# A two-layer FFN block kernel: token blocks of the FFN's up-projection formed between its products, four tile pairs begun at its start, pools that wait tile by tile, and the first value product in a score bank

## The chip, the cores and the metric

The kernel runs on one core of a Trainium2 chip, as one program. The metric is the device time of one execution in microseconds; less is better. The names are those of the profile: PE is TensorE (PEld its weight loads), DVE is VectorE, ACT is ScalarE, POOL is GpSimd, SP is SyncE, which issues nearly all DMAs here.

## The reference

Two layers over 1024 tokens of width 1024, all in float32. Layer 0 mixes with a gated MLP and a multi-scale pool (the even mixer), layer 1 with two kinds of attention (the odd mixer). After each mixer stands the same feed-forward network, of width 2816, which this change is mostly about:

```
def conv_ffn(h, w_up, conv_w, conv_b, w_down):
    a, g = jnp.split(h @ w_up, 2, axis=-1)
    a = lax.conv_general_dilated(a, conv_w, window_strides=(1,), padding=((CONV_WIDTH - 1, 0),),
                                 dimension_numbers=('NWC', 'WIO', 'NWC'), feature_group_count=D_FF) + conv_b
    return (jax.nn.gelu(a) * g) @ w_down
...
        h = h + mix
        h = h + conv_ffn(rms_norm(h, norm_ffn[layer]), ffn_w_up[layer], ffn_conv_w[layer],
                         ffn_conv_b[layer], ffn_w_down[layer])
```

## The kernel before, in words

Activations lie transposed: features on the 128 partitions, tokens along the row. A half is 512 tokens. Every product of float32 operands is made of three matmuls on a high and a low part (`mm3`, L163 to L165): high times high, high times low, low times high. `split` (L174 a cast on ACT for the high part, L175 a subtraction on DVE for the low part) makes the two parts of an activation; weights get theirs from L348 and L352 in the FFN and L133 and L134 elsewhere.

The order on each engine is fixed when the program is built: a scheduler takes the order in which the code is written and places each engine's instructions from it. On the chip an engine works through its own list in order, and semaphores hold it where data or a buffer are not ready.

**The up-projection of the FFN** takes one pair of 128-column tiles (a tile of `a`, a tile of `g`) at a time, 22 pairs, numbered j, in each layer. The four products of a 2x2 block scheme are replaced by seven (a Strassen-like scheme): the tokens are the columns, the model width is cut in two, and the two token halves give blocks. Products 1 to 7 (`PRODUCTS`, each four steps of `mm3`, so 12 matmuls of 512 columns) multiply sums of weight tiles ("forms" 0 to 3 of a pair, made on DVE and split) by sums of token blocks:

- b11 and b21: the first half's tokens, scaled by the norm, in two halves of the width. They depend on the first half of the tokens alone.
- d, e, b22, t3, t4: sums and differences that need the second half's tokens too.

Product 1 uses b11, product 2 b21, product 3 d, product 4 e, product 5 b22, product 6 t3, product 7 t4. `read` takes the results out of PSUM: product 1 is copied by ACT (L412, f_x), 2 is added to it on DVE (L419, into the `a` row f_a), 3 copied (f_z), 4 copied (f_u) from the bank that product 1 opened, 5 added (L425), 6 added (L428). After product 7 come the convolution (L434 to L437) and the gate (L442, L443), which sends the pair's result to HBM.

The blocks are formed by `apply`, called twice. The call for half 0 makes b11 and b21; the call for half 1 makes d, e, b22, t3 and t4, all of them, before `up` begins. Each starts with `Norm.stats`: eight small matmuls that sum the squares over the partitions (ps_n, L209), a square root worked out on DVE in a chain of small steps (L212, L180 to L185), a copy (n_rb, L215) and matmuls that spread the result to all partitions (ps_b, L218). Then each 128-row tile is scaled (L309) in place, and blocks of 128x1024 are added (L322 for d, L326 for e, L331 for t3, L335 for t4) and split.

In `up`, the first two pairs run together, product by product (1 of both, 2 of both, 3, 4, 5, 6, 7); from pair 2 on each pair runs alone in the order 1, 2, 4, 3, 6, 5, 7, with the next pair's forms made in between. The seven products of a pair use three PSUM banks: x is taken from the pool ps_mm (2 buffers), y and z from ps_mx (4 buffers).

**Before the first FFN** stands the even mixer's output projection (`out_proj`, ps_o); it calls `apply(0)`, then the second half's projection with `ahead` (the forms 0 and 1 of the pairs 0 and 1), then `apply(1)`. **Before the second FFN** stands the odd mixer's output projection, in the loop at the end of the program: for each half, eight accumulations (ps_o), then `ahead`, then `apply`.

**At the start of the odd mixer** (`odd_mixer`) the query and key projection (`Proj.half`, ps_qk) and the value projection (`Values.half`, ps_vv) both take their PSUM banks from ps_mm, of two buffers. ps_qk of the first half takes both; ACT copies them out (L660); then ps_vv comes. Ahead of those copies in ACT's list stand the casts (L174, `hph<-n_t`) of the second half's norm. The score banks (`ps_sc`) are of a pool of the odd mixer, and lie where the pools ps_mx0 and ps_sm0 of the stage before lay.

**Pools**: a pool that is opened where another was closed must wait until the old contents are out of use. In the kernel before, the pools of the FFN have `reuse_waits="tile"` (a tile waits for those old tiles alone that lay in its place); the others don't.

Of the kernel before, what the change touches and what calls it, by code (L numbers as in the profile page):

```python
# [18 lines left out]
P = 128  # L19
# [41 lines left out]
def tile_block(  # L61
# [22 lines left out]
    const = ctx.enter_context(tc.tile_pool(name="const", bufs=1))  # L84
    dram = ctx.enter_context(tc.tile_pool(name="dram", bufs=1, space=DRAM))
    wraw_p = ctx.enter_context(tc.tile_pool(name="wraw", bufs=2))
    wsp_p = ctx.enter_context(tc.tile_pool(name="wsp", bufs=4))
    hn_p = ctx.enter_context(tc.tile_pool(name="hn", bufs=1))
    ps_mm = ctx.enter_context(tc.tile_pool(name="ps_mm", bufs=2, space=PSUM))
# [174 lines left out]
    class FFN:  # L264
        def __init__(self, layer, stack):
            self.layer = layer
            hp = stack.enter_context(tc.tile_pool(name=f"ffh{layer}", bufs=1, reuse_waits="tile"))
            self.raw_p = stack.enter_context(tc.tile_pool(name=f"ffr{layer}", bufs=4, reuse_waits="tile"))
            self.np = tc.tile_pool(name=f"ffn{layer}", bufs=1, reuse_waits="tile")
# [21 lines left out]
        def apply(self, half):  # L291
            pb, _ = self.norm.stats(half * HF)
            H = self.H
            if half == 0:
                self.X = self.blocks("x", F32R)
            X = self.X
            self.B = {
                "b11": ([hph[m][0] for m in range(2)], [hpl[m][0] for m in range(2)]),
                "b21": ([hph[m + 2][0] for m in range(2)], [hpl[m + 2][0] for m in range(2)]),
                "b22": ([hph[m + 2][1] for m in range(2)], [hpl[m + 2][1] for m in range(2)]),  # L300
                "d": ([hph[m][1] for m in range(2)], [hpl[m][1] for m in range(2)]),
                "e": (X[0], X[1]),
                "t3": (X[2], X[3]),
            }

            def scaled(m):
                for kt in (2 * m, 2 * m + 1):
                    t = self.hT[kt][half]
                    V.scalar_tensor_tensor(t, t, pcol(PC_FFN[self.layer] + kt), pb, op0=ALU.mult, op1=ALU.mult)  # L309

            def put(name, m, src):
                hi, lo = self.B[name]
                split(hi[m], lo[m], src)

            if half == 0:
                for m in range(4):
                    scaled(m)
                    put("b11" if m < 2 else "b21", m % 2, H[m][0])
                return
# [908 lines left out]
```

## Time and profile before

| what | value |
|---|---|
| median of 3 runs | 2398.79 us |
| lowest, highest | 2397.45, 2400.97 us |
| the profiled execution's own time | 2396.34 us |
| its span, from the first to the last instruction | 2394.6 us |
| PE busy | 2307.8 us, 96% of the span |
| DVE busy | 1552.0 us, 65% |
| ACT busy | 954.8 us, 40% |
| mean granted PE clock | 0.988 |

PE is busy nearly always; the windows view tells where it is not, and where its clock was granted at less than 1.00. The first FFN's up-projection begins at about 260 us of the span, the odd mixer at about 938 us, the second FFN's at about 1685 us.

A row of the windows view gives a stretch of the span, its length, then busy time and number of instructions of PE, PEld, DVE, ACT and POOL, then the granted PE clock, the share of busy DMA engines and GB/s. A row of the timeline gives the start, the length (of a group of xN instructions, all together), the engine, the line, the operation with output and inputs and, in brackets, how long the engine sat idle before it and who released it. Matmul rows overlap, since the pipeline takes in the next while the last drains: what counts is the distance from start to start.

### The profile page before, as it was taken

What the parts mean: (1) busy time and instruction counts of PE and PEld (TensorE: products, weight loads), DVE (VectorE), ACT (ScalarE), POOL (GpSimd) and SP (SyncE); (2) the same over time, 40 slices, a digit from 0 to 9 for tenths busy, and PEclk for the clock granted to TensorE, in tenths of its full rate; (3) what the DMA queues carried; (4) which work ended last, traced back from release to release, by engine and by line L of the source; (5) the groups of instructions that cost most, each with busy time, mean ns of one, the idle gap of its engine ahead of it and who ended that gap; (6) DMA issues with size and microseconds to landing.
All of it is one profiled execution on the core that took longest, in us unless ns stands there. A gap on an engine that the chain in (4) does not pass through costs nothing.

```text
span 2394.6 us, 30695 instructions
## 1 busy us (share of the span) xinstructions
PE 2307.8 (96%) x11652; PEld 1948.4 (81%) x11652; DVE 1552.0 (65%) x2957; ACT 954.8 (40%) x1549; POOL 9.2 (0%) x67
## 2 busy tenths in 40 slices
PE   7999899999999998999999999999699999999997
PEld 7888688888888887898888888878578888888887
DVE  6663976666674447355544788896986666675446
ACT  6231433343441113445544555663444333341111
POOL 0000000000000000000000000000000000000000
PEclk9999999999999999999999999999899999999998
DMA  4114132222273213122122131233322222263211
GB/s 139 62 55 165 36 97 88 79 80 80 88 244 107 89 50 108 55 76 79 60 69 73 37 103 54 75 124 135 134 89 88 88 80 80 86 235 119 88 36 71
DMA packets 174067, 221.60 MB, mean 93 GB/s; under 512 B 11104, under 2 KB 121952, under 8 KB 173920
## 3 DMA queue, kind: packets, MB, share of 16 engines
q1 hardware_dynamic: 173056, 218.61, 28.0%
q8 instruction: 91, 1.49, 0.3%
q10 hardware_dynamic: 864, 1.04, 0.2%
q14 instruction: 56, 0.46, 0.1%
HBM read 160.79 MB, written 52.53 MB: 89 GB/s over the span
## 4 chain that ended last, share of the span: by engine, by line
PE 82%; DVE 9%; ACT 4%; DMA 3%; issue 2%; SPq 0%; DVEq 0%; ACTq 0%
PE ps_d L163 7%; PE ps_d L164 7%; PE ps_d L165 7%; PE ps_x L163 6%; PE ps_x L165 6%; PE ps_x L164 6%; PE ps_z L165 3%; PE ps_z L164 3%; PE ps_z L163 3%; PE ps_qk L163 3%; PE ps_qk L165 3%; PE ps_qk L164 3%; PE ps_o L165 2%; PE ps_o L163 2%; PE ps_o L164 2%
## 5 line engine op out<-in xcount | busy, mean ns | idle before, releaser
L163 PE MATMUL ps_d<-hph,wh 128*128 128x512 f32 (+1 forms) x736 | 279.8, 380 | 0.0
L164 PE MATMUL ps_d<-hpl,wh 128*128 128x512 f32 (+1 forms) x736 | 279.7, 380 | 0.0
L165 PE MATMUL ps_d<-hph,wl 128*128 128x512 f32 (+1 forms) x736 | 279.6, 380 | 0.0
L544 DVE TENSOR_TENSOR x<-ps_d,x 128x512 f32<-128x512 f32 (+1 forms) x200 | 131.9, 666 | 184.9 <-PE ps_d L165 184.7
L134 DVE TENSOR_TENSOR wl<-raw,wh 128x1024 fp32r<-128x1024 f32 (+1 forms) x110 | 131.9, 1200 | 172.7 <-ACT wh L133 172.5
L133 ACT CAST wh<-raw 128x1024 fp32r<-128x1024 f32 (+1 forms) x110 | 113.3, 1036 | 261.8 <-PE ps_d L164 177.3
L348 ACT CAST wh<-q 128x1024 fp32r<-128x1024 f32 x88 | 92.4, 1050 | 247.9 <-PE ps_z L164 218.9
L352 DVE TENSOR_TENSOR wl<-q,wh 128x1024 fp32r<-128x1024 f32 x88 | 107.6, 1224 | 126.7 <-ACT wh L348 126.7
L165 PEld LDWEIGHTS ps_d<-hph,wl 128*128 128x128 f32 x736 | 138.4, 188 | 26.4
L163 PEld LDWEIGHTS ps_d<-hph,wh 128*128 128x128 f32 x736 | 138.4, 188 | 26.3
L164 PEld LDWEIGHTS ps_d<-hpl,wh 128*128 128x128 f32 x736 | 138.4, 188 | 25.9
L163 PE MATMUL ps_qk<-hph,wh 128*128 128x512 f32 x384 | 151.9, 396 | 0.0
L165 PE MATMUL ps_qk<-hph,wl 128*128 128x512 f32 x384 | 151.6, 395 | 0.0
L164 PE MATMUL ps_qk<-hpl,wh 128*128 128x512 f32 x384 | 151.5, 394 | 0.0
L163 PE MATMUL ps_z<-hph,wh 128*128 128x512 f32 x352 | 139.0, 397 | 7.1 <-ACT hph L174 6.6
L163 PE MATMUL ps_x<-x,wh 128*128 128x512 f32 x352 | 137.3, 391 | 4.8 <-ACT f_u L412 4.8
L165 PE MATMUL ps_z<-hph,wl 128*128 128x512 f32 x352 | 139.3, 396 | 1.0 <-DVE wl L352 1.0
L164 PE MATMUL ps_z<-hpl,wh 128*128 128x512 f32 x352 | 139.5, 396 | 0.7 <-DVE hpl L175 0.7
L164 PE MATMUL ps_x<-x,wh 128*128 128x512 f32 x352 | 137.3, 390 | 1.0 <-DVE x L175 1.0
L165 PE MATMUL ps_x<-x,wl 128*128 128x512 f32 x352 | 136.8, 389 | 0.0
L163 PE MATMUL ps_vv<-wh,hph 128*128 128x256 f32 x384 | 110.2, 287 | 10.2 <-ACT qk L660 10.2
L164 PE MATMUL ps_vv<-wl,hph 128*128 128x256 f32 x384 | 110.7, 288 | 0.0
(268 smaller groups left out, 5511.4 us busy)
## 6 DMA issues: line engine op xcount, KB each, us to landing
wr<-in_w_up SPq DMA_DIRECT2D x88, 512.0 KB, 4.1
a_dram<-h SPq DMA_DIRECT2D x44, 512.0 KB, 2.6
ar<-a_dram SPq DMA_DIRECT2D x44, 512.0 KB, 4.6
raw<-in_w_dn SPq DMA_DIRECT2D x44, 512.0 KB, 4.5
raw<-in_w_oin SPq DMA_DIRECT2D x36, 512.0 KB, 3.7
h_dram<-h SPq DMA_DIRECT2D x32, 256.0 KB, 4.8
x<-h_dram SPq DMA_DIRECT2D x32, 256.0 KB, 5.2
raw<-in_w_ein SPq DMA_DIRECT2D x12, 512.0 KB, 4.4
```

The source lines that it names most:

```text
L133: A.copy(wh, raw)
L134: V.tensor_sub(wl, raw, wh.bitcast(F32))
L163: T.matmul(ps, lh, rh, start=first, stop=False, skip_group_check=more)
L164: T.matmul(ps, lh, rl, start=False, stop=False, skip_group_check=more)
L165: T.matmul(ps, ll, rh, start=False, stop=last, skip_group_check=more)
L348: A.copy(t[0], src)
L352: V.tensor_sub(l, src, h.bitcast(F32))
L544: V.tensor_tensor(h, ps, h, op=ALU.add)
```

## The change

1. `FFN.apply(1)` no longer forms blocks; it only gets the norm's scale. A new method `block` forms one block of one index, and `up` calls it between the products, each block just ahead of the product that uses it.
2. Pairs 2 and 3 (`early`) run their products 1 and 2, which need b11 and b21 alone, in the first group too, before product 3 of any pair; their sum is kept in a small tile and copied to the `a` row when the pair's turn comes (`open_a`). Their raw `a` tiles are loaded and split by `ahead` in place of form 1 of the pairs 0 and 1, which moves into `up`; the whole of their raw tiles is loaded again later.
3. The up-projection takes its six banks once and hands them on in a list (`self.banks`): a product that opens a bank takes the one longest free. Results are kept in two small tiles a pair instead of four: product 4 is copied into the tile that held product 1, product 6 is added in place.
4. In the second FFN both calls of `apply` follow after the projection of both halves.
5. All pools get `reuse_waits="tile"`.
6. The first value product of the odd mixer accumulates in two score banks instead of ps_mm.

```diff
+    def pool(name, **kw):
+        return tc.tile_pool(name=name, reuse_waits="tile", **kw)
...
+        def block(self, name, m):
...
+            if name == "d":
+                self.scaled(m, 1)
                 V.tensor_sub(H[m][0], H[m][0], H[m][1])
...
+                self.put("d", m, H[m][0])
+            elif name == "e":
+                self.scaled(m + 2, 1)
                 V.scalar_tensor_tensor(H[m][0], H[m][0], -1.0, H[m + 2][1], op0=ALU.mult, op1=ALU.subtract)
...
         def ahead(self, i):
-            for j in range(2):
-                self.forms_of(j, i)
+
+            for j in (2 * i, 2 * i + 1):
+                if j not in self.early:
+                    self.forms_of(j, 0)
+                    continue
+                a = wraw_p.tile([P, 1024], F32, tag="raw", name="a")
+                nc.sync.dma_start(a.rearrange("p (k c) -> p k c", c=P), self.columns(j, 0))
...
             if opens:
-                st[bank] = ps_mm.tile([P, HF], F32, tag="mm", name="ps_x") if n == 1 else ps_mx.tile(
-                    [P, HF], F32, tag="mx", name=f"ps_{bank}")
+                st[bank] = self.banks.pop(0)
...
+                to = st[1] if j in self.early else st["a"][:, 2 : 2 + HF]
+                V.tensor_tensor(to, st["y"], st[1], op=ALU.add)
+                self.banks.append(st["y"])
             elif n == 4:
-                copy("u2", "x")
+                A.copy(st[1], st["x"])
...
             both = (0, 1)
-            for n in (1, 2):
-                for j in both:
-                    self.product(j, n)
+            for j in both:
+                self.product(j, 1)
+                self.product(j, 2)
+            for j in both:
+                self.forms_of(j, 1)
+                self.block("d", j)
+                self.product(self.early[j], 1)
+                self.product(self.early[j], 2)
+            for j in both:
+                self.product(j, 3)
+            for j in both:
+                self.block("e", j)
+            for j in both:
+                self.product(j, 4)
+            for j in both:
+                self.block("b22", j)
...
-                self.product(j, 1)
+                if j in self.early:
+                    self.open_a(j)
+                else:
+                    self.product(j, 1)
...
                     vals[kind, a] = Values((V_D if kind == "d" else V_C)[a], kind == "d" and a > 0)
                     pr.half(0)
-                    vals[kind, a].half(0)
+
+                    vals[kind, a].half(0, *((ps_sc, "sc") if n == 0 else ()))
                     pr.half(1)
...
             ff.ahead(half)
+        for half in range(2):
             ff.apply(half)
```

What this makes of the engines' lists is shown at three places. Outside the starts of the two FFNs and of the odd mixer, PE, DVE and ACT have the same instructions in the same order as before. Lines of the changed kernel are a few higher (L309 is L315, L322 is L326, L326 is L330, L175 is L178, L419 is L433).

The first place is DVE in the first FFN, from the copy n_rb of the second half's norm on; hpl_1_91 and hpl_1_93 are the low parts of block d, x the tile of e, ps_u the six banks of the list. Before:

```order
L215 COPY n_rb<-n_y 128x512
L309 SCALAR_TENSOR_TENSOR h_1_1660<-h_1_1660,narrow,ps_b 128x512 x2
L309 SCALAR_TENSOR_TENSOR h_1_1662<-h_1_1662,narrow,ps_b 128x512
L322 TENSOR_TENSOR h_0_1659<-h_0_1659,h_1_1660 128x1024
L309 SCALAR_TENSOR_TENSOR h_1_1662<-h_1_1662,narrow,ps_b 128x512
L309 SCALAR_TENSOR_TENSOR h_1_1664<-h_1_1664,narrow,ps_b 128x512
L175 TENSOR_TENSOR hpl_1_91<-h_0_1659,hph_1_83 128x1024
L322 TENSOR_TENSOR h_0_1661<-h_0_1661,h_1_1662 128x1024
```

And now:

```order
L218 COPY n_rb<-n_y 128x512
L315 SCALAR_TENSOR_TENSOR h_1_1660<-h_1_1660,narrow,ps_b 128x512
L433 TENSOR_TENSOR f_a<-ps_u_2299,f_s_2316 128x512
L433 TENSOR_TENSOR f_a<-ps_u_2301,f_s_2345 128x512
L315 SCALAR_TENSOR_TENSOR h_1_1660<-h_1_1660,narrow,ps_b 128x512
L359 TENSOR_TENSOR wl<-q,wh 128x1024
L326 TENSOR_TENSOR h_0_1659<-h_0_1659,h_1_1660 128x1024
L315 SCALAR_TENSOR_TENSOR h_1_1662<-h_1_1662,narrow,ps_b 128x512 x2
L178 TENSOR_TENSOR hpl_1_91<-h_0_1659,hph_1_83 128x1024
L433 TENSOR_TENSOR f_s_2386<-ps_u_2303,f_s_2386 128x512
L326 TENSOR_TENSOR h_0_1661<-h_0_1661,h_1_1662 128x1024
```

The additions of product 2 of all four pairs (L433) and the low part of form 1 now stand between the steps of block d; before, the additions (L419) stood behind the last step of t4.

The second place is PE at the start of the second FFN: ps_n and ps_b are the two steps of the norm, hph_0_82 is block b11. Before, from the last of the second half's projection on:

```order
L165 MATMUL ps_o_14706<-hph_1_87,wl 128x512
L218 MATMUL ps_b<-ident,n_rb 128x128 x4
L163 MATMUL ps_x<-hph_0_82,wh 128x512
L164 MATMUL ps_x<-hpl_0_90,wh 128x512
L165 MATMUL ps_x<-hph_0_82,wl 128x512
```

And now:

```order
L168 MATMUL ps_o_14557<-hph_1_87,wl 128x512
L212 MATMUL ps_n<-narrow,nsum 128x1 x4
L221 MATMUL ps_b<-ident,n_rb 128x128 x4
L212 MATMUL ps_n<-narrow,nsum 128x1 x4
L166 MATMUL ps_u_14663<-hph_0_82,wh 128x512
L166 MATMUL ps_u_14665<-hph_0_82,wh 128x512
```

Both norms now begin behind the projection; before, the first half's ps_n stood among the matmuls of ps_o, and the second half's ps_n and ps_b stood behind products 1 and 2 of the pairs 0 and 1. Now the second half's ps_b stands behind product 1 of pair 2.

The third place is ACT at the start of the odd mixer: qk is the copy of ps_qk, v that of ps_vv, hph the second half's normed tokens. Before:

```order
L174 CAST hph_1_89<-n_t 128x512 x2
L660 COPY qk_6969<-ps_qk 128x512
L660 COPY qk_6970<-ps_qk 128x512
L631 DMA lb<-in_lams 128x256
L636 ACT_TABLE_LOAD
L636 ACTIVATE narrow<-narrow 128x2
L720 COPY v<-ps_vv 128x256 x2
L249 ACTIVATE r_6922<-r_6920 128x512
```

And now:

```order
L177 CAST hph_1_89<-n_t 128x512 x2
L698 COPY qk_6871<-ps_qk 128x512
L698 COPY qk_6872<-ps_qk 128x512
L669 DMA lb<-in_lams 128x256
L758 COPY v<-ps_vv 128x256 x4
L674 ACT_TABLE_LOAD
L674 ACTIVATE narrow<-narrow 128x2
L698 COPY qk_6871<-ps_qk 128x512
```

The copies of qk stay behind the same casts; all four copies of the first values now follow them at once. PE's list is the same at this place; what it waits for changes, since ps_vv no longer writes the banks that these copies empty.

More of the change, by code (lines that the diff above doesn't have):

```diff
@@ L291, in apply @@
         def apply(self, half):
-            pb, _ = self.norm.stats(half * HF)
-            H = self.H
+            self.scale, _ = self.norm.stats(half * HF)
             if half == 0:
                 self.X = self.blocks("x", F32R)
[L296 to L304, printed above, removed]
@@ L320, in apply @@
-            for m in range(2):
-                scaled(m)
+                X = self.X
+                self.B = {
+                    "b11": ([hph[m][0] for m in range(2)], [hpl[m][0] for m in range(2)]),
+                    "b21": ([hph[m + 2][0] for m in range(2)], [hpl[m + 2][0] for m in range(2)]),
+                    "b22": ([hph[m + 2][1] for m in range(2)], [hpl[m + 2][1] for m in range(2)]),
+                    "d": ([hph[m][1] for m in range(2)], [hpl[m][1] for m in range(2)]),
+                    "e": (X[0], X[1]),
+                    "t3": (X[2], X[3]),
+                }
@@ new lines, in apply, with scaled, put @@
+                for m in range(4):
+                    self.scaled(m, 0)
+                    self.put("b11" if m < 2 else "b21", m % 2, self.H[m][0])
+        def scaled(self, m, half):
+            for kt in (2 * m, 2 * m + 1):
+                t = self.hT[kt][half]
+                V.scalar_tensor_tensor(t, t, pcol(PC_FFN[self.layer] + kt), self.scale, op0=ALU.mult, op1=ALU.mult)
+        def put(self, name, m, src):
+            hi, lo = self.B[name]
+            split(hi[m], lo[m], src)
+        def block(self, name, m):
+            H = self.H
+            if name == "d":
+                self.scaled(m, 1)
@@ L357, in form @@
                 return self.lo(j, n)
-            if n == 0:
+            if j not in self.forms or n == 1 and j in self.early:
                 self.raw(j)
@@ L474, in form @@
                 def form(n, part):
-                    if nxt is not None:
+                    if nxt is not None and not (n == 0 and nxt in self.early):
                         self.form(nxt, n, part)
-                self.product(j, 1)
+                if j in self.early:
+                    self.open_a(j)
+                else:
+                    self.product(j, 1)
                 if j > 2:
                     self.form(j, 3, 1)
-                self.product(j, 2)
+                if j not in self.early:
+                    self.product(j, 2)
                 if j > 2:
@@ L562, in run @@
             self.np.__exit__(None, None, None)
-            with tc.tile_pool(name=f"ffe{self.layer}", bufs=1, reuse_waits="tile") as self.ep:
+            with pool(name=f"ffe{self.layer}", bufs=1) as self.ep:
                 self.up()
-            with tc.tile_pool(name=f"ffm{self.layer}", bufs=1, reuse_waits="tile") as np_:
+            with pool(name=f"ffm{self.layer}", bufs=1) as np_:
                 norm = Norm(np_)
@@ L706, in __init__, with half @@
                         self.dram = dram.tile([S, 256], F32, tag="v_dram", name="v_dram", bufs=2)
-                def half(self, half):
+                def half(self, half, bank=ps_mm, tag="mm"):
                     for p in range(2):
-                        ps = ps_mm.tile([P, 2, 256], F32, tag="mm", name="ps_vv")
+                        ps = bank.tile([P, 2, 256], F32, tag=tag, name="ps_vv")
                         for q in range(2):
@@ L993, in tile_block @@
             V.tensor_copy(r_col[:, q * 2 : q * 2 + 2], y[:, :2])
-    with tc.tile_pool(name="ev_v", bufs=1) as evv, tc.tile_pool(name="ev", bufs=1) as ev, tc.tile_pool(
+    with pool(name="ev_v", bufs=1) as evv, pool(name="ev", bufs=1) as ev, pool(
         name="ev2", bufs=2
```

133 lines of the change are left out of this document (62 added, 71 removed).

## The prediction

> **What bounds the kernel now.** I read the page first, then who waited for whom on PE, then the windows, and last the timelines of the stretches that stood out.
>
> ```profile
> span 2394.6 us, 30695 instructions
> PE 2307.8 (96%) x11652; PEld 1948.4 (81%) x11652; DVE 1552.0 (65%) x2957; ACT 954.8 (40%) x1549; POOL 9.2 (0%) x67
> ...
> PE ps_b L218 <- DVE n_rb L215: 12.1, 6, 8.1
> ```
>
> PE does nothing in 2394.6 - 2307.8 = 86.8 us. No change of order can win more than that plus what a lowered clock costs. The waits (total, times, longest) name a stall of 8.1 us, and the windows show where they lie; the first row is the steady state, the next three the first FFN's start, then two of the odd mixer's, four of the second FFN's:
>
> ```profile
> 380.00:400.00 20.00, 20.00 (x90) 16.57 (x89) 13.67 (x18) 7.53 (x9) 0.10 (x1) 1.00 0.25 82
> ...
> 260.00:280.00 20.00, 17.62 (x78) 14.07 (x77) 17.02 (x34) 7.65 (x9) 0.36 (x2) 0.91 0.24 77
> 280.00:300.00 20.00, 13.25 (x50) 9.02 (x49) 20.00 (x20) 10.21 (x13) 0.00 (x0) 0.92 0.00 0
> 300.00:320.00 20.00, 20.00 (x82) 16.36 (x81) 17.42 (x24) 8.54 (x9) 0.20 (x2) 0.91 0.26 84
> ...
> 940.00:960.00 20.00, 11.70 (x59) 9.31 (x57) 16.26 (x34) 6.54 (x10) 0.00 (x0) 0.89 0.35 121
> 960.00:980.00 20.00, 18.03 (x117) 17.23 (x118) 8.55 (x19) 7.54 (x13) 2.52 (x7) 0.86 0.12 28
> ...
> 1680.00:1700.00 20.00, 15.59 (x61) 11.99 (x61) 18.89 (x35) 7.78 (x9) 0.00 (x0) 0.83 0.80 273
> 1700.00:1720.00 20.00, 8.04 (x38) 6.52 (x37) 17.83 (x37) 7.03 (x9) 0.20 (x2) 0.75 0.18 52
> 1720.00:1740.00 20.00, 17.65 (x66) 13.73 (x67) 20.00 (x20) 11.23 (x14) 0.00 (x0) 0.83 0.00 1
> 1740.00:1760.00 20.00, 18.54 (x81) 14.70 (x80) 19.89 (x25) 11.41 (x12) 0.20 (x2) 1.00 0.26 80
> ```
>
> In the steady state PE has no gap, and DVE is busy 13.67 of 20 us. PE's idle time is 2.4 + 6.7 = 9.1 us at the first FFN's start, 8.3 + 2.0 = 10.3 us at the odd mixer's, 4.4 + 12.0 + 2.4 + 1.5 = 20.3 us at the second FFN's: 39.7 of the 86.8 us. In these stretches the clock is below 1.00 as well. The change touches just these three. In both FFN starts DVE is full (20.00 of 20), so it is DVE's list, not PE's, that decides.
>
> **The units.** From the first FFN's start:
>
> ```profile
> 260.44 0.39 PE L163 MATMUL ps_x<-hph,wh 128*128 128x512 f32 x1
> 260.67 0.39 PE L164 MATMUL ps_x<-hpl,wh 128*128 128x512 f32 x1
> ...
> 340.26 0.39 PE L163 MATMUL ps_x<-x,wh 128*128 128x512 f32 x1
> ...
> 268.62 0.43 DVE L215 COPY n_rb<-n_y 128x512 f32<-128x512 f32 x1
> 276.32 1.22 DVE L322 TENSOR_TENSOR h<-h,h 128x1024 f32<-128x1024 f32 x1
> 277.46 1.40 DVE L309 SCALAR_TENSOR_TENSOR h<-h,narrow,ps_b 128x512 f32<-128x512 f32 x2
> 278.77 1.22 DVE L175 TENSOR_TENSOR hpl<-h,hph 128x1024 fp32r<-128x1024 f32 x1
> 295.33 0.68 DVE L419 TENSOR_TENSOR f_a<-ps_y,f_x 128x512 f32<-128x512 f32 x1
> 295.93 1.22 DVE L175 TENSOR_TENSOR h<-h,h 128x1024 fp32r<-128x1024 f32 x1
> ```
>
> By starts, a matmul takes 260.67 - 260.44 = 0.227 us (over many), a product of twelve 2.72; a 1024-wide DVE step 1.14, a 512-wide one 0.60, a scaling 1.31 / 2 = 0.66. The row of 340.26 is product 4 of pair 3: 23 products (pairs 0 to 2, and two of pair 3) were done. 23 x 2.72 = 62.6 us, and 1.8 for ps_n and ps_b, would have put it at 324.8; 15.4 us are lost.
>
> **First FFN, step by step.** Removed: the queue of all blocks ahead of the additions (295.33 stands behind t4). Moved ahead: products 1 and 2 of pairs 2 and 3, 4 x 2.72 = 10.9 us of work that needs only b11 and b21.
> - n_rb comes later: one low part (1.14) and two additions (1.2) of forms now stand ahead of it, and 0.3 for a cast whose weight buffer frees with product 2 of pair 0. It ends at 269.05 + 2.7 = 271.7, and PE waits about 0.5 in the middle of product 2 of pair 1.
> - d was complete at 279.9, 10.9 behind n_rb. Now three additions (1.8) and a low part (1.14) stand between and one scaling less: 13.1, so 284.8. PE's eight products end at 260.44 + 21.8 + 1.8 + 0.5 = 284.5, and the second half of d is wanted 6 matmuls later: no wait. This is what the four pairs buy.
> - e: addition 0.6, two sums, two scalings, four low parts: 8.8, so 293.6. PE has product 3 twice and half of product 4 twice until 293.1: 0.5.
> - t3 and form 2: 8.6, so 302.3; PE waits 0.5 for form 2 of pair 1, not for t3.
> - t4: three additions, two short low parts, two sums, two low parts, 7.6: 309.9, its first half 308.7. PE is there at 307.3: 1.7 in two pieces.
> - Pair 2 alone: forms 1 and 2 come behind two convolutions and a gate, 0.9. From pair 3 on the forms are ready in time.
>
> Waits 4.1 us instead of 15.4: the 23rd product ends near 328.8, and the term is 340.26 - 328.8 = **11.5 us**. It can't be over 15.4.
>
> **Second FFN.**
>
> ```profile
> 1678.33 0.68 DVE L286 TENSOR_TENSOR h<-ps_o,h 128x512 f32<-128x512 f32 x1
> 1685.26 0.39 PE L165 MATMUL ps_o<-hph,wl 128*128 128x512 f32 x1
> 1690.88 0.80 PE L163 MATMUL ps_x<-hph,wh 128*128 128x512 f32 x1 [3.52 <-ACT wh L348]
> 1715.37 2.04 PE L218 MATMUL ps_b<-ident,n_rb 128*128 128x128 f32 x8 [8.09 <-DVE n_rb L215]
> 1722.20 1.22 PE L163 MATMUL ps_z<-hph,wh 128*128 128x512 f32 x2 [4.79 <-ACT hph L174]
> 1779.05 0.39 PE L163 MATMUL ps_x<-x,wh 128*128 128x512 f32 x1
> ```
>
> Here the first half's norm is moved behind the second half's additions, which costs first. From 1678.33 DVE has 14 steps of 0.60 to the first norm (1686.8), then two more, the chain (2.1), a low part and n_rb: 1691.7. ps_b at the low clock (2.04, above) ends at 1693.7, three low parts of weights at 1695.1, b11 is cast at 1697.5. So product 1 starts 6.6 us later than at 1690.88. In return the second norm's n_rb falls among eight products, not behind four: the 8.09 goes, and with it most of 4.79. From 1697.5: 62.6 for 23 products, 0.9 for ps_b, 1.7 for the low clock at the start, and waits as in the first FFN (e 1.7, form 2 and t3 0.3, t4 0.7, pair 2 1.1), 3.8: 1766.5. Against 1779.05 that is **12 us** after rounding down; the steps here are the longest and the least sure.
>
> **Odd mixer.**
>
> ```profile
> 940.17 0.68 DVE L544 TENSOR_TENSOR x<-ps_d,x 128x512 f32<-128x512 f32 x1
> 951.40 0.40 PE L165 MATMUL ps_qk<-hph,wl 128*128 128x512 f32 x1
> 961.97 0.58 PE L163 MATMUL ps_vv<-wh,hph 128*128 128x256 f32 x1 [10.17 <-ACT qk L660]
> 965.55 0.40 PE L164 MATMUL ps_vv<-wl,hph 128*128 128x256 f32 x1
> 961.34 1.06 ACT L660 COPY qk<-ps_qk 128x512 f32<-128x512 f32 x2
> ```
>
> The two banks of ps_mm are emptied by the copies at 961.34 (1.06 for both), late, and ps_vv waits for them. In the score banks it waits only for what lay there before: the last sums of ps_d, read at 940.17. So ps_vv starts right behind the last ps_qk, at 951.40 + 0.23 = 951.6 instead of 961.97: 10.3 us. From 961.97 to 965.55 stand 16 steps in 3.58 us; at half of 0.227, the tile being half as wide, they would take 1.8, so the lowered clock cost 1.7, which goes with the gap. Together **12.0 us**. What is late next: the second ps_qk needs the copies, done at 962.4, and the first values' 96 matmuls end at 951.6 + 96 x 0.119 = 963.0 (0.119 is 0.227 / 2 and a little for issue). No new wait. PE's list is the same, so nothing is overtaken; bound below zero gain, above 12.0.
>
> **What costs nothing, and its cover.** The copies of the early sums are four ACT copies of 0.59 (533.58, below), with ACT at 40%. Four raw tiles of 512 KB more are loaded over SP's queue, ahead of the other weights; DMA is busy 0.24 to 0.26 of the time in the first FFN's start and 0.00 in the stretch 280 to 300, so they fit. If the second load of those tiles were late, pair 2's form 1 would be; that is not on the path before 310. Handing on six banks in order: a pair holds three, so with one pair running three are free; in the first group two pairs and the early sums hold at most six, and there DVE's additions give back y. Pools that wait by tile can only remove waits.
>
> **Sum.** 11.5 + 12 + 12.0 = 35.5 us. Against the profiled execution's own 2396.34 (span 2394.6 and 1.7 around it) that is 2360.8; the median of the runs is 2.45 above that execution, so 2363.3, **2363**.
>
> **The clock.** The shortest gap in front of a lowered clock here:
>
> ```profile
> 275.20 0.73 PE L163 MATMUL ps_z<-hph,wh 128*128 128x512 f32 x2 [1.86 <-ACT hph L174]
> 276.46 0.79 PE L164 MATMUL ps_z<-hpl,wh 128*128 128x512 f32 x1 [0.53 <-DVE hpl L175]
> ...
> 277.48 0.63 PE L163 MATMUL ps_z<-hph,wh 128*128 128x512 f32 x1
> 277.90 0.63 PE L164 MATMUL ps_z<-hpl,wh 128*128 128x512 f32 x1
> ```
>
> After waits of 1.86 and 0.53 us the step from 277.48 to 277.90 is 0.42, not 0.227. My waits are of 0.5 to 1.7 us, with at most two near each other; each such spell costs 8 matmuls x 0.2 = 1.6 us, and there are four places (e and t4, in both FFNs): up to 6.4 us less gain. I take none in the sum, since a single wait of mine is shorter than 1.86. The Trainium skill ("TensorE: Matmul & The Clock Gate", section "Part 1: The HAM clock gate (the "warmup" mystery)") has it that TensorE falls to half its rate after at least one idle window of about 3.4 us, and comes back after about 3.4 us of steady work; by that rule my waits would cost nothing, and the sum would stay 2363. The trace does not agree: 1.86 and 0.53 us apart sufficed.
>
> **The rivals.**
>
> ```profile
> 532.15 0.68 DVE L419 TENSOR_TENSOR f_a<-ps_y,f_x 128x512 f32<-128x512 f32 x1
> 533.58 0.59 ACT L412 COPY f_u<-ps_x 128x512 f32<-128x512 f32 x1 [1.84 <-PE ps_x L165]
> 536.10 0.39 PE L163 MATMUL ps_x<-x,wh 128*128 128x512 f32 x1
> ```
>
> - *DVE and ACT in turn.* Each block's high part is cast on ACT (L174), and DVE's next step may wait for it. If each of the ten block halves of an FFN costs a hop of 0.5 us on DVE's list, that is 2 x 5 = 10 us less gain: 2373. Upper end: a whole wide cast, nearly twice the 0.59 of a copy half as wide, say 1.1 each, 22 us, 2385. For it: in 280 to 300 DVE is full and ACT at 10.21, so there is one to wait for. Against: the scheduler puts other steps of DVE between, as the first place in the order shows.
> - *All goes.* DVE keeps ahead of PE everywhere: the 15.4, as much as 16.4 in the second FFN (1779.05 - 1697.5 - 62.6 - 0.9 = 18.1, less 1.7 for the clock), and 12.0: 44 us, 2355. Against: the second FFN's first product must start later.
> - *Short waits cool the clock*, as above: 6.4 less, 2369.
> - *The banks aren't free.* The change says the first values are free of the copies. If the score banks lie on tiles that are read late (those of the second half's norm, which still runs then), or the pool still waits as a whole, the odd mixer gains nothing: 2363 + 12 = 2375. For it: the profile before shows no tile in that place waiting by tile. Against: 940.17 is the last sum.
> - *Slower: product 6 behind an addition.* In all 36 steady pairs (18 an FFN) product 4 is now copied into the tile that product 2's addition reads. So that copy (533.58) waits for the addition, which stands in DVE's list behind sums on freshly loaded weights, and product 6 takes the bank only after the copy. Today the addition ends at 532.83 and product 6 starts at 536.10; with 0.59 for the copy the slack is 536.10 - 0.59 - 532.83 = 2.7 us. If the loads came late so that the addition is 3.7 us later, each pair loses 1.0 us, 36 us, and the gain is eaten: 2399. Beyond that point the change is slower; at 4.7 us it gives 2435. Against: in the steady windows PE has no idle time and DVE 6 of 20 us free.
>
> **How the numbers follow.** A measurement of this kernel can tell 0.2%, about 4.8 us, from no change. Chances: the forecast 0.50, the hop 0.20 (my lists don't show it, DVE's full windows allow it), all gone 0.10, the cooled clock 0.10, banks not free 0.07, slower 0.03. The range: upwards it takes in the hop, the clock and the banks, and most of the hop's upper end, to 2380; downwards all gone and 3 us for DVE steps shorter than mine, 2352. Left out are the slower case, and hop and banks together, under 0.2. Every case but the last lies over 4.8 us below 2398.79; with some of the slower case near no change, faster 0.95, same 0.02, slower 0.03.
>
> **What would show it.** Right: the distance from the 23rd product's end back to the first, near 68 us in both FFNs; no wait over 2 us in the first FFN's start; ps_b's wait of 8.09 gone; ps_vv starting within 0.3 us of the last ps_qk, and the copies of qk no longer named as its releaser; windows of the steady state unchanged. Wrong: a row of PE waits on hph, x or hpl of blocks that sum to over 5 us an FFN (hop); granted clock under 0.9 at those places (clock); ps_vv waiting for a reader of an old tile (banks); small waits of product 6 for f_s in many pairs (slower). If the three stretches gain as said and the time does not, something outside them was moved, and I have missed it.

## The result, and the profile after

The changed kernel takes 2362.38 us (median of four runs, 2361.55 to 2362.85), the kernel before 2399.16 (four runs, 2397.45 to 2400.97): a ratio of 0.9846, with a 95% interval from 0.9829 to 0.9863. Forecast were 2363 us, by 35.5 us of gain. The profiled execution of the changed kernel took 2362.53 us, that of before 2396.34: 33.8 us between the two that can be compared step by step. So the sum was 1.7 us too large; the medians meet better only because before's profiled execution lay 2.8 us under its own median.

The page of the changed kernel, span and busy times, and the wait for the norm in PE's list of waits (total, times, longest):

```profile
span 2360.8 us, 30644 instructions
PE 2301.3 (97%) x11652; PEld 1943.7 (82%) x11652; DVE 1550.0 (66%) x2957; ACT 957.1 (41%) x1553; POOL 9.4 (0%) x67
...
PE ps_b L221 <- DVE n_rb L218: 10.1, 6, 6.4
```

PE now idles for 2360.8 - 2301.3 = 59.5 us instead of 86.8. Its busy time fell by 6.5 us too, though it has the same number of matmuls: that fits shorter stretches at a lowered clock (the mean granted clock is 0.994 instead of 0.988). The copies of qk are no longer among those that PE waits for. The windows that answer to those of before (the second FFN begins 23.6 us earlier, so its stretches begin at 1660):

```profile
380.00:400.00 20.00, 20.00 (x90) 16.57 (x89) 13.49 (x16) 8.11 (x10) 0.10 (x1) 1.00 0.25 79
260.00:280.00 20.00, 19.75 (x96) 16.28 (x95) 17.00 (x34) 7.19 (x9) 0.00 (x0) 1.00 0.16 52
280.00:300.00 20.00, 19.99 (x88) 15.96 (x87) 19.62 (x22) 11.30 (x16) 0.00 (x0) 1.00 0.09 27
300.00:320.00 20.00, 18.81 (x82) 14.67 (x80) 19.90 (x24) 9.55 (x12) 0.20 (x2) 1.00 0.25 80
...
940.00:960.00 20.00, 20.00 (x135) 18.53 (x134) 16.27 (x31) 9.40 (x18) 3.07 (x7) 1.00 0.07 18
...
1660.00:1680.00 20.00, 11.29 (x43) 9.27 (x42) 19.64 (x36) 10.07 (x12) 0.00 (x0) 0.58 0.67 225
1680.00:1700.00 20.00, 20.00 (x92) 16.41 (x91) 17.69 (x35) 6.45 (x9) 0.00 (x0) 0.99 0.18 52
1700.00:1720.00 20.00, 18.92 (x80) 14.37 (x79) 19.97 (x22) 11.43 (x14) 0.00 (x0) 1.00 0.07 20
```

The first FFN's start and the odd mixer's are nearly full and at full clock. The second FFN's still has one hole, 8.7 us of 20 with the clock at 0.58, and nearly none behind it. The steady state is unchanged.

The rows in which one tile's matmuls are grouped give four landmarks each, with which every kernel below can be cut into stages: the first output projection (ps_o), the first down projection (ps_d), the first scores (sc_d), the last output projection, the last down projection. Of before:

```profile
L163 PE MATMUL ps_d<-hph,wh x736: 278/389/478, 696.6 to 2379.4; 128*128 128x512 f32 x168, 128*128 128x256 f32 x16
L735 PE MATMUL sc_d<-kh,qs x96: 277/283/387, 1019.5 to 1280.9; 128*128 128x256 f32 x96
L163 PE MATMUL ps_o<-hph,wh x256: 387/389/487, 170.9 to 1684.8; 128*128 128x512 f32 x128
```

And of the changed kernel:

```profile
L166 PE MATMUL ps_d<-hph,wh x736: 278/389/486, 685.1 to 2345.7; 128*128 128x512 f32 x168, 128*128 128x256 f32 x16
L773 PE MATMUL sc_d<-kh,qs x96: 277/283/387, 995.9 to 1257.8; 128*128 128x256 f32 x96
L166 PE MATMUL ps_o<-hph,wh x256: 387/389/486, 171.0 to 1660.3; 128*128 128x512 f32 x128
```

The first FFN's stage (170.9 to 696.6, now 171.0 to 685.1) is 11.6 us shorter, the odd mixer's start (696.6 to 1019.5, now 685.1 to 995.9) 12.1. From the first scores to the last output projection 0.9 is gained, and from there to the end 9.2: 10.1 us for the second FFN. Most of the 0.9 belongs there as well: the first half's ps_n, which took 0.8 us among the last matmuls of ps_o before (from 1679.32), now stands behind them. The sum of the three is 33.8.

### The profile page after: what moved, and what is told of

Read it like the earlier page. It is cut to its first block, busy times and chain, and to the rows that moved or that the text cites. A ratio compares the mean times of both kernels' runs of the same rounds, so it can differ in the third digit from the quotient of the medians.

```text
span 2360.8 us, 30644 instructions
## 1 busy us (share of the span) xinstructions
PE 2301.3 (97%) x11652; PEld 1943.7 (82%) x11652; DVE 1550.0 (66%) x2957; ACT 957.1 (41%) x1553; POOL 9.4 (0%) x67
## 4 chain that ended last, share of the span: by engine, by line
PE 83%; DVE 8%; ACT 4%; DMA 3%; issue 2%; SPq 0%; DVEq 0%; ACTq 0%
PE ps_u L168 12%; PE ps_u L167 12%; PE ps_u L166 12%; PE ps_d L166 7%; PE ps_d L167 7%; PE ps_d L168 7%; PE ps_qk L168 3%; PE ps_qk L166 3%; PE ps_qk L167 3%; PE ps_o L166 2%; PE ps_o L168 2%; PE ps_o L167 2%; PE ps_vv L168 2%; PE ps_vv L167 2%; PE ps_vv L166 2%
## 5 line engine op out<-in xcount | busy, mean ns | idle before, releaser
L166 PE MATMUL ps_u<-hph,wh 128*128 128x512 f32 x768 | 300.2, 392 | 2.2 <-ACT hph L177 2.2
L167 PE MATMUL ps_u<-hpl,wh 128*128 128x512 f32 x768 | 299.9, 391 | 0.2 <-DVE hpl L178 0.2
L168 PE MATMUL ps_u<-hph,wl 128*128 128x512 f32 x768 | 299.9, 391 | 0.0
L166 PEld LDWEIGHTS ps_u<-hph,wh 128*128 128x128 f32 x768 | 144.6, 189 | 32.7 <-ACT hph L177 2.6
L167 PEld LDWEIGHTS ps_u<-hpl,wh 128*128 128x128 f32 x768 | 144.9, 189 | 31.5 <-DVE hpl L178 1.3
L168 PEld LDWEIGHTS ps_u<-hph,wl 128*128 128x128 f32 x768 | 144.7, 188 | 30.4 <-DVE wl L359 0.4
L168 PE MATMUL ps_u<-x,wl 128*128 128x512 f32 x352 | 137.4, 390 | 1.1 <-DVE wl L359 1.1
L167 PE MATMUL ps_u<-x,wh 128*128 128x512 f32 x352 | 137.3, 390 | 1.1 <-DVE x L178 1.1
```

Source lines behind the costliest of these rows:

```text
L166: T.matmul(ps, lh, rh, start=first, stop=False, skip_group_check=more)
L167: T.matmul(ps, lh, rl, start=False, stop=False, skip_group_check=more)
L168: T.matmul(ps, ll, rh, start=False, stop=last, skip_group_check=more)
```

## The experiments

Stage lengths in us, by these landmarks (A: first ps_o to first ps_d, the first FFN; B: to the first scores, the odd mixer's start; C: to the last ps_o; D: to the last ps_d, the second FFN). The run time is the median; the kernel before, run beside each, had medians from 2395.46 to 2396.66 in these sessions.

| kernel | A | B | C | D | span | run time |
|---|---|---|---|---|---|---|
| before | 525.7 | 322.9 | 665.3 | 694.6 | 2394.6 | 2399.16 |
| changed | 514.1 | 310.8 | 664.4 | 685.4 | 2360.8 | 2362.38 |
| changed, run again | 514.0 | 310.8 | 664.0 | 684.7 | 2358.7 | 2361.42 |
| no score banks | 514.1 | 323.7 | 665.9 | 684.7 | 2374.1 | 2374.97 |
| pools as before | 514.1 | 310.8 | 662.6 | 684.2 | 2358.1 | 2359.31 |
| no early pairs | 518.6 | 310.7 | 664.6 | 694.7 | 2372.8 | 2374.77 |
| all blocks first | 519.6 | 310.8 | 664.3 | 690.7 | 2370.6 | 2372.01 |
| norm in the loop | 514.0 | 310.8 | 665.9 | 689.2 | 2366.0 | 2367.40 |
| own tile for product 4 | 514.2 | 310.8 | 664.2 | 683.8 | 2358.4 | 2361.14 |
| sums on POOL | 517.7 | 310.7 | 664.2 | 687.5 | 2364.9 | 2367.70 |
| early forms ahead | 514.1 | 310.8 | 664.3 | 683.9 | 2359.5 | 2361.47 |
| all forms ahead | 514.1 | 310.9 | 665.0 | 685.8 | 2361.0 | 2363.07 |
| h from ACT | 514.0 | 310.9 | 664.4 | 688.6 | 2362.7 | 2365.38 |
| h from ACT, early forms ahead | 514.2 | 310.7 | 664.2 | 689.0 | 2364.5 | 2365.76 |

A and B repeat to 0.2 us where a kernel does the same there. Between kernels that do the same there, C differs by up to 3.3 us and D by up to 1.6, so less than that is not read from them.

**The changed kernel again.**

> The changed kernel as it is, on the chip of the two kernels below, to set them against. All theories: a span of 2359 to 2361, and the waits of the second FFN's start as before: 6 us at ps_b, 2 us at hph, 1 us at x.

2361.42 us, a ratio of 0.9856 to the kernel before (0.9842 to 0.9871). The waits at the second FFN's start are 5.67, 2.16 and 1.07 us, as expected.

**No score banks.**

```
-                    vals[kind, a].half(0, *((ps_sc, "sc") if n == 0 else ()))
+                    vals[kind, a].half(0)
```

> The changed kernel with one edit undone: the first value product takes its banks from ps_mm again. Theory (the three places are independent, and the odd mixer's 12.0 us come from the banks alone): span 2360.8 + 12.0 = 2372.8, ps_vv waits about 10.2 us for the copies of qk again and then runs some 3.5 us at the lower clock; both FFN starts are as in the changed kernel. Rival (the tile-wise pools or something else in that stage give a part of it): the span rises by under 9 us. Both FFNs' shifts are read from the gates.

PE's timeline shows the old wait again:

```profile
949.87 0.58 PE L166 MATMUL ps_vv<-wh,hph 128*128 128x256 f32 x1 [10.18 <-ACT qk L698]
950.25 0.42 PE L167 MATMUL ps_vv<-wl,hph 128*128 128x256 f32 x1
950.47 0.41 PE L168 MATMUL ps_vv<-wh,hpl 128*128 128x256 f32 x1
```

B is 12.9 us longer than the changed kernel's (323.7 to 310.8), A the same; the steps at the lowered clock (0.22 us from 950.25 to 950.47, where 0.12 is the pace at full clock) are back as well. With everything else as in the changed kernel, B is no shorter than before the change (322.9): the odd mixer's 12 us come with the banks alone.

**The pools as before.**

```
+        if name.startswith("ff"):
+            kw["reuse_waits"] = "tile"
-        return tc.tile_pool(name=name, reuse_waits="tile", **kw)
+        return tc.tile_pool(name=name, **kw)
```

> The changed kernel with the pools outside the FFN waiting as a whole again; the score banks stay. Theory: the score banks lie where the old norm's banks lay, and that norm's ps_b is read by DVE until about 949.4 in the changed kernel's trace, so ps_vv waits from 940.1 to about 949.5 and meets the lower clock: 9.3 + 1.7 = 11 us, span near 2372; the bank edit needs the pool edit. Rival (the banks alone do it; in my prediction tile-wise pools were an item that costs and brings nothing by itself): span 2360.8, within 1 us.

My theory of this run fell; the rival holds, though the span, 2358.1, lies 2.7 us under its 2360.8 and not within 1. PE goes from ps_qk to ps_vv without a gap:

```profile
939.97 0.40 PE L170 MATMUL ps_qk<-hph,wl 128*128 128x512 f32 x1
940.20 0.28 PE L168 MATMUL ps_vv<-wh,hph 128*128 128x256 f32 x1
```

B is 310.8 as in the changed kernel. I had placed the score banks on ps_sm0's room as well, and the run shows no wait for ps_b of the old norm. A likely reason, not shown by the profile, is that the three score banks lie on the four banks of ps_mx0 alone. The pool edit gains nothing. It may even cost a little: all four executions (2358.30 to 2359.77 us) lie below the eight of the changed kernel (2360.07 to 2363.15), by 2.1 us between this median and that of the changed kernel run again; in the profiles most of the difference lies in C, where kernels that do the same differ by more, so it is not traced to a cause. The prediction's "cost nothing" holds to about 2 us, its rival "the banks aren't free" falls.

**No early pairs.**

```
-        early = (2, 3)
+        early = ()
...
-                self.forms_of(j, 1)
                 self.block("d", j)
-                self.product(self.early[j], 1)
-                self.product(self.early[j], 2)
```

(`ahead` makes the forms 0 and 1 of the pairs 0 and 1 again.)

> The changed kernel without the early pairs: form 1 of the pairs 0 and 1 is made before the up-projection again, blocks are still formed between the products. Theory (both halves of the edit count, the early pairs more): PE ends four products 10.9 us earlier and then waits some 8 us for block d, at a lower clock after it; DVE reaches t4 about 3.5 us earlier; 7 us more for each FFN (5 to 9), span near 2375. Rival 1 (the order of the blocks brings nearly all): 1 to 3 us in all. Rival 2 (the early pairs bring nearly all): 20 us and more, back to the FFN starts of the kernel before.

The first FFN loses 4.5 us, the second 9.3: 13.8, against 14 expected. That the sum fits is luck, since neither of the two lies in its 5 to 9. PE's waits, first at the first FFN's block d, then at the second's n_rb and block d:

```profile
275.65 1.22 PE L166 MATMUL ps_u<-hph,wh 128*128 128x512 f32 x2 [3.38 <-ACT hph L177]
```

```profile
1695.03 2.05 PE L221 MATMUL ps_b<-ident,n_rb 128*128 128x128 f32 x8 [2.64 <-DVE n_rb L218]
1702.64 1.22 PE L166 MATMUL ps_u<-hph,wh 128*128 128x512 f32 x2 [5.56 <-ACT hph L177]
```

In the first FFN d is waited for 3.4 us, not 8: without the early pairs' additions and with form 1 made earlier DVE reaches d sooner (the low part of its second half starts 110.0 us after the first ps_o, in the changed kernel 112.8). In the second PE waits for the norm and then for d, and D is 694.7, as long as before the change (694.6): there the other parts bring nothing without the early pairs.

**All blocks first.**

```
+            for name in ("d", "e", "b22", "t3", "t4"):
+                for j in both:
+                    self.block(name, j)
+            for n in (3, 4):
+                for j in both:
+                    self.product(j, n)
...
```

> The changed kernel with the early pairs, but with all five blocks formed in one go after the early products, and forms 2 and 3 behind them. Theory: t4 no longer costs its 1.6 us, but form 2 stands behind t4's low part on DVE, at about 304 where product 5 wants it at 296: about 8 us of waiting and some lowered clock, so 6 us more for each FFN, span near 2373. Rival (early pairs bring nearly all): under 2 us each, span under 2365.

5.5 and 5.3 us longer, where 6 each were expected, and by the wait that was named: product 5 waits for form 2 (wl), which stands behind the blocks on DVE. From the first FFN:

```profile
297.11 0.49 PE L167 MATMUL ps_u<-x,wh 128*128 128x512 f32 x1 [1.35 <-DVE x L178]
301.65 0.80 PE L168 MATMUL ps_u<-hph,wl 128*128 128x512 f32 x1 [4.05 <-DVE wl L359]
```

So of the first FFN's 11.6 us, 7.1 are left without the early pairs and 6.1 with all blocks first: each part works alone, and the two overlap a little. Of the 9.2 us in D of the second, nothing is left without the early pairs and 3.9 with all blocks first. The handing on of the six banks was not taken back by itself in any run; its share is not known.

**The norm in the loop.**

```
             ff.ahead(half)
-        for half in range(2):
             ff.apply(half)
```

> The changed kernel with the second FFN's norm of the first half called inside the loop again, right behind the first half's projection, as in the kernel before. Theory (DVE is full from the second half's additions to t4, so the order decides only when PE waits, not how long in all): product 1 starts some 6.7 us earlier, the second half's n_rb comes some 2 us later and block d is waited for about 10 us, with a second spell at the lower clock: span 0 to 4 us over 2360.8, likeliest 2. Rival (the late start of product 1, 6.7 us, is a cost that the split loop alone causes): span about 2355.

5.0 us slower than the changed kernel's median, 3.8 of them in D. The span is 5.2 us longer, so the theory had the direction, but its range (0 to 4) was too narrow; the rival, faster by 6, is out. PE's waits:

```profile
1663.47 1.13 PE L221 MATMUL ps_b<-ident,n_rb 128*128 128x128 f32 x8 [0.64 <-DVE n_rb L218]
1668.12 0.79 PE L166 MATMUL ps_u<-hph,wh 128*128 128x512 f32 x1 [3.52 <-ACT wh L355]
...
1694.62 2.04 PE L221 MATMUL ps_b<-ident,n_rb 128*128 128x128 f32 x8 [6.44 <-DVE n_rb L218]
1698.10 0.79 PE L166 MATMUL ps_u<-hph,wh 128*128 128x512 f32 x1 [1.44 <-DVE f_a L433]
```

The last ps_o starts at 1662.4 here and product 1 follows 5.7 us later, in the changed kernel 13.3 us (1660.75 to 1674.03). The 7.6 us are given back at the second norm, 6.44 + 1.44, and the lowered clock takes some more (the second spell). It is n_rb that is late, not block d as I had put it.

**A tile of its own for product 4's copy.**

```
             elif n == 4:
-                A.copy(st[1], st["x"])
+                st[4] = ep.tile([P, HF], F32, tag="sb", name="f_s4", bufs=6)
+                A.copy(st[4], st["x"])
```

(Product 5's addition reads it.)

> The changed kernel with a tile of its own for product 4's copy, so that the copy no longer waits for product 2's addition. Theory (the slack of 2.7 us in the 36 steady pairs hides that wait): the same within 0.5 us, 2360.8. Rival (product 6 waits a little in many pairs): faster by 36 x 0.1 = 3.6 us or more.

2361.14 us against 2362.38 and 2361.42: the same; a small wait in each of the 36 pairs would have shown. In one of these pairs in the changed kernel's trace the addition ends before the copy can start, so that the copy waits for PE alone:

```profile
520.59 0.68 DVE L433 TENSOR_TENSOR f_a<-ps_u,f_s 128x512 f32<-128x512 f32 x1
...
522.05 0.59 ACT L436 COPY f_s<-ps_u 128x512 f32<-128x512 f32 x1 [1.85 <-PE ps_u L168]
```

**Four tries at what is left.** The second FFN's start still costs some 12 us (8.7 idle in 1660 to 1680, and 3.1 at the lowered clock, as worked out below), so I looked for a faster version there.

The sums of squares on POOL:

```
-                V.tensor_add(self.sums[c0], self.sums[c0], sq)
+                self.eng.tensor_add(self.sums[c0], self.sums[c0], sq)
...
-            self.norm = Norm(self.np.__enter__())
+            self.norm = Norm(self.np.__enter__(), G)
```

> The changed kernel with the FFN norms' sums of squares (L205, seven additions a half) on POOL in place of DVE. Theory (what is left of the FFN starts is DVE's list): DVE loses 14 steps of 0.60, 8.4 us, ahead of each FFN; in the second FFN the first n_rb comes 2 to 3 us earlier and weight parts are made sooner: 2 to 5 us less there, in the first FFN up to 1.5 us less, since only 2.4 us of waits are left; span 2354 to 2358. Rival (an addition on POOL takes over 1.36 us, the pace of the projection's tiles, or slows DVE beside it): the chain of seven sums ends later than on DVE and n_rb with it, span over 2361.

Slower, 2367.70 us, as the rival had it. POOL's timeline, in the first FFN, then all fourteen of the second:

```profile
263.84 1.99 POOL L206 TENSOR_TENSOR nsum<-nsum,nsq 128x512 f32<-128x512 f32 x1 [2.02 <-ACT nsq L205]
...
1650.06 18.92 POOL L206 TENSOR_TENSOR nsum<-nsum,nsq 128x512 f32<-128x512 f32 x14 [695.67 <-ACT nsq L205]
```

An addition takes 1.35 (18.92 / 14) to 2.0 us against 0.60 on DVE. In the first FFN, PE's ps_n waits 3.3 us for the sums, and A is 3.6 longer. In the second an addition does not take more than the rival's 1.36 us, but its other condition is met: beside POOL's additions, which end at 1668.92, four of the norm's small steps on DVE took 0.57 to 1.13 us (from 1664.38 to 1669.0), where the same steps take 0.16 in the changed kernel and 0.16 again from 1669.03 on.

The early pairs' forms ahead of the last projection:

```
         w = load_w(w_ooutb)
+        ff.ahead(1)
         for half in range(2):
...
-            ff.ahead(half)
+            if half == 0:
+                ff.ahead(0)
```

> The changed kernel with the early pairs' forms 0 (raw tiles loaded by 1636, weight buffers free from about 1640) made ahead of the last projection in the second FFN; the forms of the pairs 0 and 1 stay behind its first half. Theory (the second FFN's start is bound by DVE's list, and DVE and ACT do nothing for most of 1632 to 1645): two low parts of 1.14 us leave the full stretch, the first n_rb is not earlier but what follows it is: 1 to 2.3 us less than the changed kernel. Rival (the start is bound by the loads of h and the chain of the norm, not by DVE's list): no change beyond 0.5 us, or later, when the two weight buffers that pairs 0 and 1 took now come only at the projection's end.

2361.47 us to 2361.42 of the changed kernel run again: nothing. The wait for b11's cast falls from 2.16 to 1.08 us, as the theory had it, but the one for n_rb is 6.43, against 5.67 in the changed kernel run again and 6.40 in its first profile. So at most 1 us is gained at that place, less than these runs can tell apart.

All forms ahead of it (`ff.ahead(0)` stands beside `ff.ahead(1)`):

> As the kernel with the early pairs' forms 0 ahead, but with the forms of the pairs 0 and 1 also called ahead of the last projection: their raw tiles are loaded ahead of the stores of h, and their casts stand between the squares of the last tiles on ACT. Theory: 1 to 2 us more gained than by the early pairs' alone, since the weights no longer land behind the norm. Rival (ACT waits at those casts for weight buffers that come free at the projection's end, and the last squares and n_rb wait behind): 1 to 3 us slower than with the early pairs' alone.

2363.07 us, 1.6 slower than with the early pairs' forms alone: the rival's size, but not its mechanism. The first n_rb is waited for 9.6 us instead of 5.7. ACT waits for only 0.3 us at the two casts; on DVE two low parts of weights (1.14 each, at 1661.40 and 1663.14) now stand ahead of the norm's first step n_v, which starts at 1666.08 (1663.17 in the changed kernel), and n_rb follows at 1670.99 (1667.75). So here it is DVE's list that holds n_rb.

The loads of h from ACT, and with them the early forms. The first of the two kernels also moves both calls of `ahead` behind the whole projection, so it changes two things:

```
-                nc.sync.dma_start(ff.hT[kt][half], h_dram[...])
+                (A if half == 0 else nc.sync).dma_start(ff.hT[kt][half], h_dram[...])
...
-            ff.ahead(half)
         for half in range(2):
+            ff.ahead(half)
+        for half in range(2):
             ff.apply(half)
```

> The changed kernel with the eight loads of h for the first half before the second FFN issued from ACT, which does nothing there from 1632 to 1646, in place of SP, where they stand behind two stores that wait until 1641.5; the weight forms are called behind the projection. Theory (the start of the second FFN hangs on the chain load of h, addition, sums, norm): the first addition starts at 1641 to 1643 in place of 1645.5, the first n_rb comes 2 to 3 us earlier, and so does what follows: span 2 to 3 us less than the changed kernel. Rival (the end of the projection and the second half's additions decide, or the stream of loads of 4 MB takes as long whoever issues it): under 1 us.

> The same loads from ACT, and the early pairs' forms 0 made ahead of the projection. Theory (once the chain is earlier, DVE's list is what is left): 1 to 2 us less than with the loads alone, 3 to 5 us less than the changed kernel. Rival (DVE's list is not the bound in that place, as with the early forms alone): no different from the loads alone by over 0.5 us.

Both slower, 2365.38 and 2365.76 us: the theory was right on the first steps and wrong on the rest. DVE's list in the first of them:

```profile
1640.14 1.28 DVE L289 TENSOR_TENSOR h<-ps_o,h 128x512 f32<-128x512 f32 x2
...
1661.03 0.15 DVE L215 TENSOR_SCALAR n_v<-ps_n 128x4 f32<-128x4 f32 x1
...
1665.60 1.23 DVE L359 TENSOR_TENSOR wl<-wr,wh 128x1024 fp32r<-128x1024 f32 x1 [3.69 <-ACT wh L355]
```

The additions start at 1640.14, 5 us earlier, and the norm's first step (n_v) at 1661.03, 2.1 earlier. But a weight part got a place ahead of the norm's chain in DVE's list, and its raw tile is late: SP issues the stores of h first, and the cast on ACT waits for the load.

```profile
1649.65 8.62 SPq L291 DMA_DIRECT2D h_dram<-h  x13
...
1664.53 1.04 ACT L355 CAST wh<-wr 128x1024 fp32r<-128x1024 f32 x1 [3.95 <-DMA wr<-in_w_up]
```

In the changed kernel SP issues all four loads of weights (1656.97) ahead of the last eight stores (1663.68). So the late weight part points to the moved calls of `ahead` rather than to the loads of h from ACT. What those loads bring with the calls left in place was not run, and that the order on SP bounds the changed kernel's own start is not shown. No kernel tried here beats the changed one by over 0.2%.

## Why the prediction was right, point by point

**First FFN: 11.5 forecast, 11.6 measured**, and step by step. DVE's rows of the changed kernel:

```profile
271.30 0.43 DVE L218 COPY n_rb<-n_y 128x512 f32<-128x512 f32 x1
...
283.80 1.23 DVE L178 TENSOR_TENSOR hpl<-h,hph 128x1024 fp32r<-128x1024 f32 x1 [0.38 <-ACT hph L177]
...
292.53 1.22 DVE L178 TENSOR_TENSOR x<-h,x 128x1024 fp32r<-128x1024 f32 x1
...
300.02 2.35 DVE L178 TENSOR_TENSOR x<-h,x 128x1024 fp32r<-128x1024 f32 x2
...
307.75 2.35 DVE L178 TENSOR_TENSOR h<-h,h 128x1024 fp32r<-128x1024 f32 x2
```

n_rb ends at 271.7 (forecast 271.7), d at 283.80 + 1.14 = 284.9 (284.8), e at 293.7 (293.6), t3 at 302.3 (302.3), t4 at 310.0 (309.9). Where the list is full, its steps can be added up. PE's waits behind it:

```profile
307.88 0.50 PE L166 MATMUL ps_u<-h,wh 128*128 128x512 f32 x1 [0.56 <-DVE f_s L441]
309.02 0.50 PE L167 MATMUL ps_u<-h,wh 128*128 128x512 f32 x1 [0.63 <-DVE h L178]
320.89 0.50 PE L168 MATMUL ps_u<-x,wl 128*128 128x512 f32 x1 [0.53 <-DVE wl L359]
328.74 0.39 PE L166 MATMUL ps_u<-x,wh 128*128 128x512 f32 x1
```

The two pieces at t4 and the one at pair 2 are there; the 0.5 at e and at t3 are not, and n_rb is waited for 0.25. The last row is product 4 of pair 3, the landmark of the forecast: 328.74 for 328.8. That PE's side fits so well is in part luck. From product 1 at 260.54 it is 68.2 us: 62.6 for 23 products, 1.7 for ps_n and ps_b, 2.0 of waits, and 1.9 in single steps longer than 0.227, most of them next to the waits. The forecast had 4.1 of waits and no term for longer steps; its two errors cancel.

**Odd mixer: 12.0 forecast, 12.1 measured.** ps_vv starts 0.23 us behind the last ps_qk, as forecast:

```profile
939.92 0.39 PE L168 MATMUL ps_qk<-hph,wl 128*128 128x512 f32 x1
940.15 0.28 PE L166 MATMUL ps_vv<-wh,hph 128*128 128x256 f32 x1
```

The second half's wait that I said would not arise does not: its ps_qk starts at 951.66, right behind the first values. The run without the banks took 12.9 back.

**Second FFN: 12 forecast (12.5 before rounding down), 10.1 measured**, the one term that was mis-sized; it makes the 1.7 us of the sum. PE's rows:

```profile
1668.32 2.05 PE L221 MATMUL ps_b<-ident,n_rb 128*128 128x128 f32 x8 [6.40 <-DVE n_rb L218]
1674.03 1.22 PE L166 MATMUL ps_u<-hph,wh 128*128 128x512 f32 x2 [2.16 <-ACT hph L177]
...
1679.40 0.63 PE L167 MATMUL ps_u<-hpl,wh 128*128 128x512 f32 x1
1711.85 0.50 PE L167 MATMUL ps_u<-x,wh 128*128 128x512 f32 x1 [1.08 <-DVE x L178]
1725.07 0.50 PE L167 MATMUL ps_u<-h,wh 128*128 128x512 f32 x1 [0.45 <-DVE h L178]
1737.54 0.50 PE L168 MATMUL ps_u<-x,wl 128*128 128x512 f32 x1 [0.53 <-DVE wl L359]
1745.39 0.39 PE L166 MATMUL ps_u<-x,wh 128*128 128x512 f32 x1
```

Product 1 starts at 1674.03 + 23.6 = 1697.6 in before's time (forecast 1697.5), and the waits behind it (1.08, 0.45, 0.53 and one of 0.15) make 2.2, less than the 3.8 allowed for. But from product 1 to the 24th product it takes 1745.39 - 1674.03 = 71.4 us, not 69.0. The lowered clock holds until 1679.8 (steps of 0.43 for 0.227): about 3.1 us lost where 1.7 was taken. The rest, 2.5 us, lies mostly in single steps of 0.3 to 0.45 us, for which the sum had no term; here no error of the other sign makes up for them.

**The rivals.** The hop between DVE and ACT: single waits of DVE for a cast are there (0.38 at 283.80), but no 0.5 for each of ten, since the scheduler puts other steps between. All gone: no, product 1 of the second FFN starts late as said. Banks not free, and product 6 behind an addition: the runs above speak against both. The cooled clock: the waits of 0.56 and 0.63 within 1.2 us, at 307.88 and 309.02, cost none of it (the clock is 1.00 in 300 to 320). It fell after 6.40 and 2.16 us here, and after 3.38 and 4.05 us in the experiments, whose clocks over those 20 us were:

```profile
260.00:280.00 20.00, 16.29 (x69) 12.51 (x69) 17.28 (x33) 6.37 (x8) 0.00 (x0) 0.87 0.22 66
```

```profile
300.00:320.00 20.00, 18.35 (x71) 14.93 (x72) 18.50 (x24) 9.12 (x11) 0.10 (x1) 0.84 0.32 90
```

(the first without early pairs, the second with all blocks first). The rule of the Trainium skill ("TensorE: Matmul & The Clock Gate", section "Part 1: The HAM clock gate (the "warmup" mystery)"), at least one idle window of about 3.4 us, agrees with these. Two places don't fit it: the 1.86 and 0.53 us of the kernel before, with two matmuls between them, and, in the second FFN with all blocks first, waits of 1.76 and 2.72 us with four matmuls between them, after which the steps were 0.43 us (clock 0.75 in 1720 to 1740). In these, waits near each other lowered the clock though neither was that long by itself.

## What to carry to other kernels

Where an engine's list is full, its times could be forecast here to a tenth of a microsecond by adding up steps in the order of the new list. What is left to guess is the clock behind an idle stretch, the slightly longer steps of the engine that waits on that list (1.9 and 2.5 us here), and the stages where several lists and loads meet. Work that needs only what is ready (here the early pairs) and the order of the work that it waits for (here the blocks) belong together: in the second FFN the order paid nothing without the early pairs, and they paid less than half without the order. And 12 of the 34 us came from an edit of one call that moved an accumulation to banks that lay unused.

## What the runs showed of the hardware that I had not expected

- The granted clock was recorded as 0.944 for the whole execution with the norm in the loop, 0.95 in windows where PE did exactly what it does at 1.00 in the changed kernel: in 400 to 600 us both have 200.00 us of PE busy with x884 matmuls, and the first FFN took 514.0 us in one, 514.1 in the other. A clock that is a few per cent lower throughout is not evidence of lost time by itself.
- An addition of 128x512 on POOL took 1.35 us in a row of fourteen, and 1.3 to 2.0 us by itself, against 0.60 on DVE; and while POOL added, small steps on DVE took up to 1.13 us instead of 0.16.
- Several waits near each other lowered PE's clock where none was as long as the 3.30 us (sums on POOL) and 3.38 us (no early pairs) that did so alone: 1.86 and 0.53 us in one place, 1.76 and 2.72 in another. Waits of 0.56 and 0.63 us within 1.2 us did not.
- The same program's two profiles differ by 0.7 us in the second FFN's stage (685.4 and 684.7). The spell at the lowered clock is alike, ten steps of 0.43 us in a row in each; what differs is the wait for n_rb, 6.40 and 5.67 us.
